# A two-layer decoder trunk: two adaptive-norm rounds moved to layer 1, one overflow loop, roots by threes

## The chip, the cores and the metric

The kernel runs on one core of a Trainium2 chip. The metric is the device time of one execution in microseconds (us). Engines: TensorE (PE in the rows; PEld is its weight load), VectorE (DVE), ScalarE (ACT), GpSimd (POOL), SyncE (SP). SP issues most loads and stores, ACT and POOL some.

## The reference

One sequence of 1,024 tokens, width 1,024, float32, two layers. Each layer takes shift, scale and gate for its two halves from a condition vector `c` ("adaptive norm": a matrix of 1,024 x 6,144 per layer). Layer 0's mixer joins a gated delta rule with a sparse attention that keeps the top 256 keys of each query; layer 1's is a gated linear attention. Behind each mixer stands a mixture of 32 experts, two for each token. At the end there is one more norm. Shortened:

```python
def reference(x, c, ...):
    for layer in range(2):
        shift1, scale1, gate1, shift2, scale2, gate2 = split(silu(c) @ ada_w[layer] + ada_b[layer], 6)
        h = rms_norm(x, norm_mix[layer]) * (1 + scale1) + shift1
        x = x + gate1 * (even_mixer(h) if layer == 0 else gla_mixer(h))
        h = rms_norm(x, norm_ffn[layer]) * (1 + scale2) + shift2
        x = x + gate2 * hier_moe(h)
    return rms_norm(x, final_norm)
```

## The kernel before

Tokens go in eight tiles of 128. A float32 product is made of three products of rounded parts: weights are loaded (`wraw`, `raw`), rounded on ACT (`whi`, `mhi`) and the rest formed on VectorE (`wlo`, `mlo`); TensorE then multiplies hi by hi, lo by hi and hi by lo (`mm3`, L112 to L114).

**Order.** Most of the program is written as generators that are advanced in turn, and a scheduler orders each engine's instructions from that; within an engine they run in that order, and waits for other engines are semaphores. Loads go in order of issue on the queue of their engine.

**Adaptive norm.** `ada_steps` (L263) works in rounds `(layer, g)`, g = 0, 1, 2, each a third of a layer's 6,144 columns: 16 tiles of 128 x 1,024 (`adaw`, 512 KB, loaded by POOL from `later`, L475, into two buffers), each multiplied in four matmuls (eight records in the trace) with `cond` at L283. At a round's start ACT loads the bias (L275); at its end VectorE adds it (L289), and for g > 0 ACT stores the row to `mods` in DRAM (L295), from where `gtf` is read later. Rounds (0,1), (0,2), (1,0), (1,1) and (1,2) run inside layer 0's projections (list at L473), one tile after each projected tile of rotary queries or keys. There VectorE and ACT also search the attention's thresholds bit by bit (`count`, L683 and L685; step at L701, L702), and VectorE applies the rotation (L494 to L497), TensorE turns the result (`tp`, L605) and ACT stores it (`qo`).

**Overflow loop.** Each expert takes 128 tokens in the main pass. What is over goes through a loop (L1703) whose count is read from the device. A turn fetches one expert's six weight parts by indirect loads on POOL (`fetch`, L1685), multiplies, and leaves `y`; the rows of `y` are scattered to `ybuf` (`scatter`, L1533) at the head of the next turn, with the indices `xic` kept from before, so the first turn's scatter carries none, and a second loop of at most one turn (L1719) makes the last scatter.

**Layer 1's norm stage** (`odd_mix`, L1787 to L1825). For each tile `combine` (L1740) loads the two expert rows (`yt`, 1 MB, four buffers), weighs and adds them (L1745 to L1748); `normalise` (L325, L328) makes `xn`, TensorE transposes it (L348) to `hh`, `hl`; `gate` multiplies it with the group `w3` of the weights, and two tiles later with `w0`. SP asks for `gtf`, then `yt`, then the weights of `w3`, whose rest `wlo` is formed on POOL (L370).

**The end** (`final`, L2060). Tile by tile: ACT scales (L2086), VectorE joins (L2090 to L2092), ACT squares (L2096), VectorE takes the root (eight short operations, L123 to L134) and multiplies (L2107); tile 6's product is on ACT and POOL (L2104, L2105). The order on these three engines is the order of the code.

Of the kernel before, what the change touches and what calls it, by code (L numbers as in the profile page):

```python
# [9 lines left out]
F32 = mybir.dt.float32  # L10
# [12 lines left out]
P = 128  # L23
# [4 lines left out]
NE = 32  # L28
# [59 lines left out]
class Trunk:  # L88
# [173 lines left out]

    def ada_steps(self, rounds, wp, pp, load, wait):  # L263

# [4 lines left out]
        for layer, g in rounds:  # L269
# [4 lines left out]
            for j in range(4):  # L274
                nc.scalar.dma_start(bias[32 * j:32 * j + 32].rearrange("p (u c) -> p u c", u=2), bcast(b2[j], 32))  # L275
            ps = pp.tile([P, 512], F32, name="ada", bufs=1)
            for u in range(2):
# [14 lines left out]
            if g:  # L292
# [3 lines left out]
                continue  # L296
            pt = pp.tile([P, 512], F32, name="ada", bufs=1)
            for c in range(4):
# [100 lines left out]
    def even_keep(self, st):  # L399
        nc = self.nc  # L400
        kp = self.pool(st, "keep0")
        self.cond = kp.tile([P, KD, 32], F32, name="cond")
        self.blk = kp.tile([P, 16], F32, name="blk")
# [16 lines left out]
    def even_inproj(self):  # L420
# [51 lines left out]
        self.rope_tables(hp)  # L472
        rounds = [(0, 1), (0, 2), (1, 0), (1, 1), (1, 2)]  # L473

# [933 lines left out]
    def moe(self, layer):  # L1408
        nc, tc, d = self.nc, self.tc, self.d
        tt, ts, stt, act, mm, tr = self.tt, self.ts, self.stt, self.act, self.mm, self.tr  # L1410
        with ExitStack() as st:
# [280 lines left out]
            y = y_tile()  # L1692
            nc.gpsimd.memset(ixc, 1 << 20)
            nc.gpsimd.memset(y, 0.0)
            for x in lw:
# [7 lines left out]
            with tc.For_i(0, nv, 1) as _:  # L1703
                scatter(y, ixc[:, 0:1])
                for n in range(2, 6):
                    fetch(n)
                x = all_tokens(xgs[0])
                w1 = take(0)
                p1 = up(x, w1)
                nc.vector.tensor_copy(ixc, ixn)  # L1710
                find()
                fetch(0)
                fetch(1)
                pick()
                p3 = up(x, take(1))
                h = hidden(gated(silu(p1), p3))
                down(h, take(2), y)
            any = nc.values_load(nx[0:1, 1:2], min_val=0, max_val=1)
            with tc.For_i(0, any, 1) as _:  # L1719
                scatter(y, ixc[:, 0:1])  # L1720
# [3 lines left out]
    def overflow(self, kp, sp):  # L1724
# [3 lines left out]
        xi = kp.tile([P, NE], I32, name="xi")  # L1728
        n = kp.tile([P, 2], I32, name="nx")
        ts(xb, self.base[:, NT], -1.0, 0.0, op0=OP.add, op1=OP.max)  # L1730
# [3 lines left out]
        nc.vector.tensor_tensor_scan(xc, self.ones[:, :NE], xb, 0.0, op0=OP.mult, op1=OP.add)  # L1734
        nc.vector.tensor_copy(n[:, :1], xc[:, NE - 1:NE])
        ts(n[:, 1:], xc[:, NE - 1:NE], 1.0, None, op0=OP.min)
        tt(xb, xc, xb, op=OP.subtract)
# [14 lines left out]
    def odd_mix(self):  # L1752
# [34 lines left out]
        with ExitStack() as sx:  # L1787
            xp = self.pool(sx, "x1p")
            junk = xp.tile([P, D], BF, name="junk")

            gt = xp.tile([P, D], F32, name="gtf")
            nc.sync.dma_start(gt, self.mod_row(0, 5))

            def tiles(ids):
                xs = [self.combine(xp, j, 4, gt) for j in ids]
                ys = [xp.tile([P, D], F32, name="xn", bufs=2) for _ in ids]
                self.normalise(xp, xs, junk, ys)
                return ys

            w3 = []  # L1800

            def get(i):
                if i:
                    yield from tiles((i, i + 1))
                    return
                yield from tiles((0,))
                w3.append(load(nc.gpsimd.tensor_tensor))
                with nullcontext():
                    yield from tiles((1,))

            norm = self.mixer_norm(1, get, xp, pp, "tp", hh, hl)
            next(norm)
            nc.scalar.dma_start(gn[:, :256], bcast(d["gla_out_norm"][0], P))
            nc.scalar.dma_start(gn[:, 256:], bcast(d["gla_out_norm"][0, :16], P))
            w0 = load()
            for i in range(NT + 2):
                if i % 2 == 0:
                    next(norm, None)
                if i < NT:
                    gate(3, w3[0], i)  # L1820
                if i >= 2:
                    gate(0, w0, i - 2)
                    nc.sync.dma_start(self.x2[(i - 2) * P:(i - 1) * P, :], self.xs[i - 2])
                if i == NT - 1:
                    ahead = load()  # L1825
        self.xst.close()
        before = self.rst
# [232 lines left out]
def final(k):  # L2060
# [3 lines left out]
    with ExitStack() as st:  # L2064
# [4 lines left out]
        gt = fp.tile([P, D], F32, name="gtf")  # L2069
        nc.sync.dma_start(gt, k.mod_row(1, 5))  # L2070
        yts = []
        for i in range(NT):
            yt = fp.tile([P, 2, D], F32, name="yt", bufs=NT)
            nc.sync.dma_start(yt, k.ybuf[i * 2 * P:(i + 1) * 2 * P, :].rearrange("(p k) d -> p k d", k=2))
            yts.append(yt)
        fn = fp.tile([P, D], F32, name="fng")
        p = pp.tile([P, D], F32, name="fn")
# [23 lines left out]
        def norm(i):  # L2101
            o = outs[i]
            if i == 6:
                k.act(o, k.xs[i], AF.Copy, scale=rs[:, i:i + 1])  # L2104
# [3 lines left out]
            nc.sync.dma_start(k.out[0, i * P:(i + 1) * P, :], o)  # L2108

        with k.tc.manual_schedule(engines={EN.DVE, EN.Activation, EN.Pool}):  # L2110
            scale(0)
            join(0)
            for i in range(NT):
                if i + 1 < NT:
                    scale(i + 1)
                square(i)
                root(i, i + 1)
                if i + 1 < NT:
                    join(i + 1)
                norm(i)  # L2120
    k.xst.close()
    k.rst.close()
# [28 lines left out]
```

## Time and profile before

| what | value |
|---|---|
| median of 3 runs | 2948.32 us (2944.62 to 2948.60) |
| the profiled execution | 2950.39 us, span 2948.7 us |
| granted TensorE clock, mean | 0.942 |
| TensorE busy | 2617.1 us, 89% |
| VectorE busy | 2218.7 us, 75% |
| ACT busy | 1690.3 us, 57% |
| POOL busy | 544.8 us, 18% |
| moved by DMA | 683.08 MB, mean 232 GB/s |

The span runs from the first to the last instruction. A busy share is a mean over stages; which engine sets the pace is read stage by stage. In the rows, "x8" is a count, `out<-in` names the tiles, and the bracket at a row's end is the engine's idle time before it and what ended that.

### The profile page before, as it was taken

How to read it: one execution, taken by the hardware profiler on the slowest of the kernel's cores; microseconds unless marked ns; L12 is line 12 of the kernel's file. 1: busy time of each engine (PE TensorE's matmuls, PEld its weight loads, DVE VectorE, ACT ScalarE, POOL GpSimd, SP SyncE). 2: the span in 40 equal slices, each digit the busy share in tenths (PEclk: the TensorE clock that was granted, in tenths of full speed). 3: DMA queues.
4: the chain of work that ended last, by engine and by line, in shares of the span. 5: the costliest groups of instructions: out<-in, count | busy, mean ns of one | idle time of the engine just before them, and what ended most of it. 6: DMA issues, size and time to landing. Idle time of an engine off the chain costs nothing. (4 is left out here: it accounts for less than half of the span.)

```text
span 2948.7 us, 46535 instructions
## 1 busy us (share of the span) xinstructions
PE 2617.1 (89%) x17622; PEld 2119.0 (72%) x17622; DVE 2218.7 (75%) x4055; ACT 1690.3 (57%) x2168; POOL 544.8 (18%) x511
## 2 busy tenths in 40 slices
PE   5999998877898899999997479999997999999980
PEld 3667887756687688888885367789786788888860
DVE  6777669577766899999986563483476999999866
ACT  4456653233444577777774456255433777777762
POOL 0100111232210122222223310002001122222220
PEclk8999999888999899999998779999997999999995
DMA  6345665422124799999994543444635899999964
GB/s 232 103 127 172 203 192 164 126 80 75 49 100 158 281 368 376 377 383 378 367 356 177 181 148 104 153 156 131 225 124 202 338 367 377 379 380 376 364 238 178
DMA packets 230569, 683.08 MB, mean 232 GB/s; under 512 B 50277, under 2 KB 128953, under 8 KB 176842
## 3 DMA queue, kind: packets, MB, share of 16 engines
q1 hardware_dynamic: 161696, 548.14, 50.8%
q0 software_dynamic: 37424, 107.01, 10.6%
q10 hardware_dynamic: 31226, 24.97, 2.6%
q8 instruction: 138, 2.26, 0.3%
q14 instruction: 85, 0.70, 0.1%
HBM read 628.07 MB, written 94.40 MB: 245 GB/s over the span
## 5 line engine op out<-in xcount | busy, mean ns | idle before, releaser
L1435 DVE TENSOR_TENSOR mlo<-raw,mhi 128x2048 fp32r<-128x2048 f32 (+1 forms) x420 | 915.1, 2194 | 96.0 <-ACT mhi L1434 94.8
L1434 ACT ACTIVATE mhi<-raw 128x2048 fp32r<-128x2048 f32 (+1 forms) x420 | 768.0, 1844 | 93.1 <-PE y L114 45.7
L112 PE MATMUL h<-mhi,xh 128*128 128x512 f32 x1072 | 434.2, 405 | 4.3 <-ACT xh L1496 2.7
L113 PE MATMUL h<-mlo,xh 128*128 128x512 f32 x1072 | 429.1, 400 | 4.6 <-DVE mlo L1435 4.6
L114 PE MATMUL h<-mhi,xl 128*128 128x512 f32 x1072 | 428.2, 399 | 0.0
L112 PE MATMUL pj<-whi,hh 128*128 128x256 f32 (+2 forms) x1088 | 325.5, 299 | 12.6 <-ACT hh L356 12.5
L114 PE MATMUL pj<-whi,hl 128*128 128x256 f32 (+2 forms) x1088 | 316.8, 291 | 4.1 <-DVE hl L357 4.1
L113 PE MATMUL pj<-wlo,hh 128*128 128x256 f32 (+2 forms) x1088 | 316.5, 291 | 0.0
L1483 POOL DMA_INDIRECT xg<-hbuf,tix x64 | 135.1, 2110 | 685.4 <-PE tp L1494 464.1
L113 PEld LDWEIGHTS h<-mlo,xh 128*128 128x128 f32 x1072 | 204.5, 191 | 52.5 <-DVE mlo L1435 6.7
L112 PEld LDWEIGHTS h<-mhi,xh 128*128 128x128 f32 x1072 | 204.7, 191 | 51.8 <-ACT xh L1496 4.0
L114 PEld LDWEIGHTS h<-mhi,xl 128*128 128x128 f32 x1072 | 204.2, 190 | 49.1 <-DVE xl L1497 0.9
L112 PEld LDWEIGHTS pj<-whi,hh 128*128 128x128 f32 x1088 | 210.7, 194 | 37.6 <-issue 18.1
L112 PE MATMUL y<-mhi,hh 128*128 128x512 f32 x536 | 224.2, 418 | 7.1 <-ACT mhi L1434 5.1
L113 PE MATMUL y<-mlo,hh 128*128 128x512 f32 x536 | 213.9, 399 | 3.4 <-DVE mlo L1435 3.4
L114 PEld LDWEIGHTS pj<-whi,hl 128*128 128x128 f32 x1088 | 209.7, 193 | 7.6 <-DVE hl L357 5.7
L114 PE MATMUL y<-mhi,hl 128*128 128x512 f32 x536 | 214.0, 400 | 0.9 <-DVE hl L1526 0.9
L113 PEld LDWEIGHTS pj<-wlo,hh 128*128 128x128 f32 x1088 | 210.7, 194 | 2.7 <-issue 1.3
L1533 POOL DMA_INDIRECT ybuf<-y,yix x64 | 145.6, 2276 | 195.7 <-ACT y L1545 169.2
L1496 ACT ACTIVATE xh<-tp 128x512 fp32r<-128x512 f32 x134 | 79.4, 597 | 124.6 <-PE tp L1494 124.6
L112 PE MATMUL pj<-hh,whi 128*128 128x512 f32 x320 | 130.0, 406 | 0.0
L370 DVE TENSOR_TENSOR wlo<-wraw,whi 128x512 fp32r<-128x512 f32 (+2 forms) x104 | 72.4, 708 | 75.4 <-ACT whi L369 75.1
(714 smaller groups left out, 5083.8 us busy)
## 6 DMA issues: line engine op xcount, KB each, us to landing
raw<-in_exp_w_dram SPq DMA_DIRECT2D x380, 1024.0 KB
adaw<-in_ada_w_dram POOLq DMA_DIRECT2D x80, 512.0 KB, 4.4
yt<-ybuf SPq DMA_DIRECT2D x16, 1024.0 KB
wraw<-in_even_w_in_dram SPq DMA_DIRECT2D x48, 256.0 KB
x<-in_x_dram SPq DMA_DIRECT2D x16, 512.0 KB
aw<-in_ada_w_dram SPq DMA_DIRECT2D x8, 1024.0 KB
hbuf<-th SPq DMA_DIRECT2D x16, 512.0 KB
x<-x SPq DMA_DIRECT2D x16, 512.0 KB
```

The lines of the kernel that those rows point to most:

```text
L112: self.mm(ps, ah, bh, start=first, stop=False)
L113: self.mm(ps, ah, bl, start=False, stop=False)
L114: self.mm(ps, al, bh, start=False, stop=last)
L370: (take or self.tt)(lo[:, ks, :cols], raw[:, :, :cols], hi[:, ks, :cols].bitcast(F32), op=OP.subtract)
L1434: act(h[:, us], raw[:, us], AF.Copy)
L1435: (take[u] if take else tt)(l[:, us], raw[:, us], h[:, us].bitcast(F32), op=OP.subtract)
L1483: return nc.gpsimd.indirect_dma_start(out=xg, out_offset=None, in_=self.hbuf, in_offset=bass.IndirectOffsetOnAxis(ap=it, axis=0), bounds_c ...
L1496: act(xh[:, us], as4(p), AF.Copy)
L1533: return nc.gpsimd.indirect_dma_start(out=self.ybuf, out_offset=bass.IndirectOffsetOnAxis(ap=iy, axis=0), in_=y, in_offset=None, bounds_ch ...
```

## The change

Rounds (1,1) and (1,2) leave layer 0's projections and run in layer 1's norm stage: six tiles are stepped after the first tiles of the norm have been put in the program, then three in each turn of the loop over tiles, the rest after it. `cond` moves to the pool that lives throughout; `yt` has three buffers instead of four. `w3` is loaded first in that stage, and split on VectorE. The overflow loop ends with its own scatter; the second loop, two memsets and a column of `nx` go. In `final` the first `yt` is asked for ahead of `gtf`, roots are taken for tiles 0 to 2, 3 to 5 and 6 to 7, and tile 5's product instead of tile 6's is on ACT and POOL.

```diff
@@ layer 0, projections
-        rounds = [(0, 1), (0, 2), (1, 0), (1, 1), (1, 2)]
+        rounds = [(0, 1), (0, 2), (1, 0)]
@@ overflow loop
             y = y_tile()
-            nc.gpsimd.memset(ixc, 1 << 20)
-            nc.gpsimd.memset(y, 0.0)
...
             with tc.For_i(0, nv, 1) as _:
-                scatter(y, ixc[:, 0:1])
                 for n in range(2, 6):
                     fetch(n)
...
                 down(h, take(2), y)
-            any = nc.values_load(nx[0:1, 1:2], min_val=0, max_val=1)
-            with tc.For_i(0, any, 1) as _:
                 scatter(y, ixc[:, 0:1])
@@ odd_mix
+            rounds = [(1, 1), (1, 2)]
+
+            def later(i):
+                x = xp.tile([P, 1024], F32, name="adaw", bufs=2)
+                nc.gpsimd.dma_start(x, self.ada_tile(i, rounds))
+                return x
+
+            ada = self.ada_steps(rounds, xp, pp, later, 0, "a", 3)
+            next(ada)
+
+            w3 = load()
             gt = xp.tile([P, D], F32, name="gtf")
             nc.sync.dma_start(gt, self.mod_row(0, 5))
 
             def tiles(ids):
-                xs = [self.combine(xp, j, 4, gt) for j in ids]
+                xs = [self.combine(xp, j, 3, gt) for j in ids]
...
-            w3 = []
-
             def get(i):
-                if i:
-                    yield from tiles((i, i + 1))
-                    return
-                yield from tiles((0,))
-                w3.append(load(nc.gpsimd.tensor_tensor))
-                with nullcontext():
-                    yield from tiles((1,))
+                return tiles((i, i + 1)) if i else itertools.chain.from_iterable(map(lambda j: tiles((j,)), (0, 1)))
 
             norm = self.mixer_norm(1, get, xp, pp, "tp", hh, hl)
             next(norm)
+            w0 = load()
+            for _ in range(6):
+                next(ada)
...
-            w0 = load()
             for i in range(NT + 2):
...
                 if i == NT - 1:
                     ahead = load()
+                for _ in range(3):
+                    next(ada, None)
+            run(ada)
@@ final
-        nc.sync.dma_start(gt, k.mod_row(1, 5))
...
             yts.append(yt)
+            if i == 0:
+                nc.sync.dma_start(gt, k.mod_row(1, 5))
...
-            if i == 6:
+            if i == 5:
...
+        after = {3: (root, 0, 3), 4: (norm, 0), 5: (norm, 1), 6: (norm, 2)}
         with k.tc.manual_schedule(engines={EN.DVE, EN.Activation, EN.Pool}):
             scale(0)
-            join(0)
             for i in range(NT):
                 if i + 1 < NT:
                     scale(i + 1)
+                join(i)
                 square(i)
-                root(i, i + 1)
-                if i + 1 < NT:
-                    join(i + 1)
+                if i in after:
+                    f, *j = after[i]
+                    f(*j)
+            root(3, 6)
+            for i in range(3, 6):
                 norm(i)
+            root(6, 8)
+            norm(6)
+            norm(7)
```

What this does to the order of instructions shows at three places. In layer 0's projections, TensorE: `pj` are the projection's matmuls, `tp` the transposes of the rotated tile, `ada` the adaptive norm's.

```order
 L114 MATMUL pj<-whi,hl 128x256
 L605 MATMUL tp<-ident,qa 128x128 x2
-L283 MATMUL ada<-adaw,cond 32x256 x4
 L112 MATMUL pj<-whi,hh 128x256
 L113 MATMUL pj<-wlo,hh 128x256
```

The four matmuls of one ada tile go; 32 such places are left out of this stretch.

POOL in the overflow loop, before; L1533 is the scatter, L1685 a fetch:

```order
L1533 DMA ybuf<-y,xic 2048x1024 [waits DMASW5_49,DMASW4_49,Pool_49]
L1685 DMA raw<-in_exp_w_dram,xw 128x2048 [waits DMASW6_49]
L1685 DMA raw<-in_exp_w_dram,xw 128x2048
L1685 DMA raw<-in_exp_w_dram,xw 128x2048 [waits DMASW0_49]
L1685 DMA raw_15477<-in_exp_w_dram,xw 128x2048 [waits DMASW1_49]
L1685 DMA raw<-in_exp_w_dram,xw 128x2048 [waits DMASW2_49,DVE_49,Activation_49]
L1685 DMA raw<-in_exp_w_dram,xw 128x2048 [waits DVE_49,Activation_49]
L1483 DMA xg_10377<-hbuf,xin 128x1024 [waits DVE_49,PE_49]
```

and with the change:

```order
L1685 DMA raw<-in_exp_w_dram,xw 128x2048 [waits DMASW5_49,Pool_49]
L1685 DMA raw<-in_exp_w_dram,xw 128x2048 [waits DMASW6_49,Pool_49]
L1685 DMA raw<-in_exp_w_dram,xw 128x2048 [waits DMASW7_49,Pool_49]
L1685 DMA raw_15262<-in_exp_w_dram,xw 128x2048 [waits DMASW0_49,Pool_49]
L1685 DMA raw<-in_exp_w_dram,xw 128x2048 [waits DMASW1_49,DVE_49,Activation_49]
L1685 DMA raw<-in_exp_w_dram,xw 128x2048 [waits DMASW2_49,DVE_49,Activation_49]
L1483 DMA xg_10163<-hbuf,xin 128x1024 [waits DMASW3_49,DVE_49,PE_49]
L1533 DMA ybuf<-y,xic 2048x1024 [waits DMASW4_49,Activation_49]
```

The scatter has gone from the head, where it waited for earlier POOL loads, to the foot, where it waits for ACT's `y`; the loop's closing branch, which waits for all loads and stores, comes right behind it.

TensorE at the start of layer 1's norm stage, before; `tp` transposes the first tile's `xn`, `pj` is its gate product:

```order
L348 MATMUL tp<-ident,xn 128x128 [waits DVE_49]
L348 MATMUL tp<-ident,xn 128x128 x7
L112 MATMUL pj<-whi,hh 128x260 [waits Activation_49]
L113 MATMUL pj<-wlo,hh 128x260 [waits Pool_49]
L114 MATMUL pj<-whi,hl 128x260 [waits DVE_49]
```

and with the change, from the end of the tenth ada tile on:

```order
L283 MATMUL ada<-adaw,cond 32x256 [waits DMASW6_49]
L283 MATMUL ada<-adaw,cond 32x256 x3
L283 MATMUL ada<-adaw,cond 32x256 [waits DMASW7_49]
L348 MATMUL tp<-ident,xn 128x128 [waits DVE_49]
L348 MATMUL tp<-ident,xn 128x128 x7
L283 MATMUL ada<-adaw,cond 32x256 x3
L283 MATMUL ada<-adaw,cond 32x256 [waits DMASW0_49]
L283 MATMUL ada<-adaw,cond 32x256 x3
L283 MATMUL ada<-adaw,cond 32x256 [waits DMASW1_49]
L283 MATMUL ada<-adaw,cond 32x256 x3
L112 MATMUL pj<-whi,hh 128x260 [waits Activation_49]
L113 MATMUL pj<-wlo,hh 128x260
```

The first thing that TensorE does there is now ten ada tiles, each behind its load; the transposes and the gate products of the first tiles stand between and behind further ada tiles, 22.25 of the 32 ahead of the third tile's `pj`. On POOL, 17 of the tile loads stand ahead of the first gate product `z`.

## Rows read from the trace of the kernel before

**Rows 1.** The page's slices, TensorE: busy tenths, 40 equal slices of the span.

```profile
PE   5999998877898899999997479999997999999980
```

**Rows 2.** Windows, layer 0's projections: us; busy PE, PEld, DVE, ACT, POOL; clock; DMA; GB/s.

```profile
390.00:410.00 20.00, 20.00 (x182) 17.01 (x184) 11.51 (x45) 13.34 (x25) 2.65 (x5) 1.00 0.58 166
...
470.00:490.00 20.00, 15.61 (x134) 11.30 (x126) 19.12 (x36) 2.31 (x6) 3.13 (x7) 0.91 0.58 174
...
sum 136.00, PE 128.45 PEld 108.48 DVE 106.85 ACT 57.87 POOL 15.85; mean PE 18.35 PEld 15.50 DVE 15.26 ACT 8.27 POOL 2.26
```

**Rows 3.** Timelines, layer 0's overflow loop: POOL, then ACT; start, duration, idle before, releaser.

```profile
1573.52 0.99 POOL L1533 DMA_INDIRECT ybuf<-y,yix  x1 [5.15 <-ACT y L1545]
1576.86 0.97 POOL L1533 DMA_INDIRECT ybuf<-y,xic  x1 [2.34 <-DMA ybuf<-y,yix]
1578.14 1.11 POOL L1685 DMA_INDIRECT raw<-in_exp_w_dram,xw  x1 [0.30 <-issue]
...
1605.58 1.06 ACT L1434 ACTIVATE mhi<-raw 128x1024 fp32r<-128x1024 f32 x1 [1.83 <-PEq L1703]
```

**Rows 4.** Timeline, SP, start of layer 1's norm stage.

```profile
1668.93 0.33 SPq L1792 DMA_DIRECT2D gtf<-mods  x1
...
1669.78 2.04 SPq L368 DMA_DIRECT2D wraw<-in_gla_w_in_dram  x3
```

**Rows 5.** Windows, layer 1's norm stage and the work behind it.

```profile
1669.00:1730.00 61.00, 16.85 (x76) 14.79 (x77) 48.29 (x89) 29.75 (x49) 9.65 (x6) 0.56 0.77 269
1730.00:1780.00 50.00, 48.94 (x391) 47.77 (x391) 23.24 (x51) 22.79 (x47) 12.84 (x16) 0.97 0.20 59
```

**Rows 6.** Timeline, TensorE, layer 1's norm stage, first transposes and third tile.

```profile
1691.58 1.97 PE L348 MATMUL tp<-ident,xn 128*128 128x128 f32 x8 [28.47 <-DMA wraw<-in_gla_w_in_dram]
...
1730.91 0.57 PE L112 MATMUL pj<-whi,hh 128*128 128x260 f32 x1
```

**Rows 7.** Timeline, VectorE, the end.

```profile
2888.88 1.28 DVE L2090 SCALAR_TENSOR_TENSOR yt<-yt,wts 128x1024 f32<-128x1024 f32 x1 [24.13 <-ACT yt L2086]
...
2893.91 0.15 DVE L123 TENSOR_SCALAR fr0y<-fss 128x1 f32<-128x1 f32 x1 [1.22 <-ACT fo L2096]
...
2895.44 1.28 DVE L2090 SCALAR_TENSOR_TENSOR yt<-yt,wts 128x1024 f32<-128x1024 f32 x1
...
2937.33 3.24 DVE L2092 TENSOR_TENSOR x<-x,yt 128x1024 f32<-128x1024 f32 x1
...
2943.45 1.28 DVE L2107 SCALAR_TENSOR_TENSOR fo<-x,frs,fng 128x1024 f32<-128x1024 f32 x1
```

**Rows 8.** Groups by line, TensorE, 366 to 470 us: count, busy us, mean ns, idle before.

```profile
L283 PE MATMUL ada<-adaw,cond 128*32 128x256 f32 x207 | 16.7, 393 | 3.1 <-DVE col L301 3.0 <-DMA adaw<-in_ada_w_dram 0.2
```

**Rows 9.** Timeline, TensorE, layer 0's projections, one period.

```profile
413.35 0.38 PE L605 MATMUL tp<-ident,qa 128*128 128x128 f32 x2
...
417.16 0.38 PE L605 MATMUL tp<-ident,qa 128*128 128x128 f32 x2
```

**Rows 10.** Groups by line, VectorE, 370 to 470 us.

```profile
L494 DVE TENSOR_TENSOR qa<-pj,cos 128x256 f32<-128x256 f32 x24 | 10.1, 420 | 9.0 <-DMA qbT<-qo 5.3 <-PE pj L114 2.7 <-ACT jka L685 0.8
```

**Rows 11.** SP at the second overflow loop's line in layer 1, and its next load.

```profile
L1719 SPq COMPARE_BRANCH  x3: 33/33/39, 2876.9 to 2880.6; - x3
...
2880.79 0.33 SPq L2070 DMA_DIRECT2D gtf<-mods  x1
```

**Rows 12.** DMA issues, 366 to 470, 450 to 492, 2300 to 2850 us: count, KB, landing us.

```profile
adaw<-in_ada_w_dram POOLq DMA_DIRECT2D x25, 512.0 KB, 4.1
...
adaw<-in_ada_w_dram POOLq DMA_DIRECT2D x10, 512.0 KB, 4.0
...
xg<-hbuf,tix POOLq DMA_INDIRECT x27, 9.2
```

**Rows 13.** Groups by line, POOL and VectorE, 1669 to 1740 us.

```profile
L370 POOL TENSOR_TENSOR wlo<-wraw,whi 128x520 fp32r<-128x520 f32 x4 | 8.2, 2078 | 14.0 <-DMA wraw<-in_gla_w_in_dram 12.3 <-ACT whi L369 1.7
...
L328 DVE TENSOR_SCALAR xn<-x,nrs 128x1024 f32<-128x1024 f32 x7 | 5.1, 746 | 0.0
```

More of the change, by code (lines that the diff above doesn't have):

```diff
@@ L261, in cond_setup, with ada_steps @@
         self.mods = self.dram.tile([2, 6 * D], F32, name="mods")
-    def ada_steps(self, rounds, wp, pp, load, wait):
+    def ada_steps(self, rounds, wp, pp, load, wait, tag="ada", bufs=1):
         nc, cp = self.nc, self.cp
@@ L275, in ada_steps @@
                 nc.scalar.dma_start(bias[32 * j:32 * j + 32].rearrange("p (u c) -> p u c", u=2), bcast(b2[j], 32))
-            ps = pp.tile([P, 512], F32, name="ada", bufs=1)
+            ps = pp.tile([P, 512], F32, name="ada", tag=tag, bufs=bufs)
             for u in range(2):
@@ L296, in ada_steps @@
                 continue
-            pt = pp.tile([P, 512], F32, name="ada", bufs=1)
+            pt = pp.tile([P, 512], F32, name="ada", tag=tag, bufs=bufs)
             for c in range(4):
@@ L401, in even_keep @@
         kp = self.pool(st, "keep0")
-        self.cond = kp.tile([P, KD, 32], F32, name="cond")
+        self.cond = self.cp.tile([P, KD, 32], F32, name="cond")
         self.blk = kp.tile([P, 16], F32, name="blk")
@@ L1728, in overflow @@
         xi = kp.tile([P, NE], I32, name="xi")
-        n = kp.tile([P, 2], I32, name="nx")
+        n = kp.tile([P, 1], I32, name="nx")
         ts(xb, self.base[:, NT], -1.0, 0.0, op0=OP.add, op1=OP.max)
@@ L1734, in overflow @@
         nc.vector.tensor_tensor_scan(xc, self.ones[:, :NE], xb, 0.0, op0=OP.mult, op1=OP.add)
-        nc.vector.tensor_copy(n[:, :1], xc[:, NE - 1:NE])
-        ts(n[:, 1:], xc[:, NE - 1:NE], 1.0, None, op0=OP.min)
+        nc.vector.tensor_copy(n, xc[:, NE - 1:NE])
         tt(xb, xc, xb, op=OP.subtract)
@@ L1819, in odd_mix @@
                 if i < NT:
-                    gate(3, w3[0], i)
+                    gate(3, w3, i)
                 if i >= 2:
```

## The prediction

> **What bounds the kernel now.** I read the page's slices first, then one table of windows for each stage that the change touches, then timelines inside these. TensorE is busy in nearly every slice [rows 1]; the three dips are the places between layers, at slice 22 to 23 (layer 0's overflow loop and layer 1's norm stage) and at the end. The change leaves both long expert stretches alone, so only four places count, and each has a limit of its own.
>
> *Layer 0's projections, 366 to 506 us.* TensorE has no gap in 390 to 410, VectorE has [rows 2]; from 470 it turns round, VectorE 19.12 of 20 and TensorE 15.61. So TensorE sets the pace first, VectorE (the threshold search and its masks) after.
>
> *Overflow loop.* It runs three times in layer 0 (three scatters of `ybuf<-y,xic` inside it, the first in [rows 3]) and not once in layer 1.
>
> *Layer 1's norm stage.* Its start is SP's `gtf` at 1668.93 [rows 4]. Until 1730 TensorE is busy 16.85 of 61 us at a granted clock of 0.56, waiting for the norm chain; from 1730 it is busy 48.94 of 50 [rows 5]. The change of limit is at 1730.91, the first `pj` of the third tile [rows 6].
>
> *The end.* VectorE works through eight tiles in a row and everything else follows it [rows 7].
>
> **Part 1: 32 ada tiles leave layer 0's projections.** The 207 records before 470 cost 16.7 us, 16.7 x 8/207 = 0.64 us for a tile's eight records [rows 8]; one sits in each TensorE period of 3.81 us (`tp` at 413.35 and at 417.16, [rows 9]). If TensorE alone set the pace, 16 us would go. VectorE's idle time speaks for it: `L494` waited 9.0 us in this stretch, and where a store of `qo` is named, the matmuls `pj` that it reads ended last, since TensorE had no gap there [rows 10]. Against the full gain: in the whole 136 us VectorE is busy 106.85 [rows 2], and it ends the stretch, so its own order (search, rope, masks) can take back a part. Bounds: -16 (all) and -3 (only the wait named for `pj`, 2.7). I take -11, nearer to the full gain, because the row without a gap is the first half of the stretch. Removed POOL issues, bias loads and stores of `mods` on ACT lie beside this and cost nothing.
>
> **Part 2: one overflow loop.** Before, the loop began with a scatter that waited 2.34 us for the last ordinary scatter, took 0.97, and the fetch behind it started at 1578.14 [rows 3]. Now the fetch is first: -3 in the first turn. The other two turns lose a scatter of 1.0 and 0.3 ahead of the fetch: -2.6. But the scatter now stands behind the turn's last `y`, and the loop's closing branch waits for it. A boundary took 1.83 us [rows 3]; a scatter needs 3.34 us from start to landing (1573.52 to 1576.86), so two boundaries get about 2 us longer, +4. On leaving, the second loop and its scatter go, -1. Sum -2.6, rounded to -3, bounds -6 and +2. The two memsets that go lay beside the experts' matmuls.
>
> **Part 3: the second loop of layer 1.** It is skipped, but SP spent 2876.9 to 2880.6 in it, and `gtf`, the first load of the end, follows at 2880.79 [rows 11]. All engines pass there, no work covers it: -3.9. Bounds -3.9 and 0 (if the wait only moves to the remaining loop).
>
> **Part 4: the same 32 tiles in layer 1's norm stage.** TensorE's order has 22.25 of them ahead of the third tile's `pj`, ten ahead of the first transposes. The idle TensorE has room for the matmuls, so the question is how fast tiles arrive. Two buffers: a tile is asked for when the tile two places earlier has been used, so two tiles take one landing plus one tile's matmuls. At clock 0.56 these take 0.64/0.56 = 1.1. Landing: 4.1 us in layer 0's projections [rows 12], 9.2 for POOL's 512 KB gathers beside saturated expert loads [rows 12]. I take 5.3, nearer to the first, since it is the same direct load, and raise it because the stage already has DMA engines busy 0.77 of the time and 269 GB/s [rows 5]. A tile then takes (5.3+1.1)/2 = 3.2, 22.25 tiles 71 us, against the 62 us that the stage had (1668.93 to 1730.91): +9. The other 9.75 tiles fall where TensorE has no gap: 9.75 x 0.64 = +6.4. In all +16. Bounds: with a landing of 4.1 a tile takes 2.6, the 22.25 are there in 58 us and only +6.4 is left; with 9.2 it is 5.15, 115 us, +59. The first weights asked for first, and their split on VectorE instead of POOL (8.2 us for four on POOL, [rows 13], beside which VectorE's own work stalled), go with this: SP now issues three weight loads ahead of the first `yt`, 2.04 us [rows 4], VectorE takes four splits of its own length and loses the stall; I cost both at nothing, because the first transposes wait for ten ada tiles (10 x 3.2 = 32 us), where they started 22.65 us into the stage (1691.58, [rows 6]). On POOL 17 tile issues stand ahead of the first gate product `z`; behind `z` waits only its store. ACT's bias loads and `mods` stores, some 16 issues, lie in a stage where ACT is busy 29.75 of 61 us [rows 5].
>
> The rows on VectorE show one more thing that touches POOL's loads: `L328`, SBUF to SBUF in f32, takes 746 ns for 1024 columns, less than 1.28 us for the two-input operation of the same size [rows 7, 13]. The Trainium skill (SBUF — State Buffer, the warning on the "DVE blocks DMA" trap) says that while VectorE runs such a two-port operation GpSimd can't write descriptors of the loads that it issues, and gives 620 ns growing to about 3,100. By that, as an estimate, a landing would be 2.5 us later, 7.8 in this stage, a tile 4.45, the part +44 and the kernel slower. The trace speaks against so much: the seven such operations here are 5.1 us in all, and while VectorE was busy 19.1 of 20 us in layer 0 the tiles still landed in 4.0 [rows 2, 12]. It stays as one cause of rival B.
>
> **Part 5: the end.** A period is 6.55 us (2888.88 to 2895.44): 3.8 for three operations, 1.22 waiting for ACT's square, 1.53 for the root's eight, or 1.28 for the norm in the wait's place. Before, 55.85 us from 2888.88 to the last norm's end at 2944.73 [rows 7]. After: 8 x 3.8 = 30.4; three roots of ten operations, about 1.9 each, 5.7; seven norms of 1.3, 9.1; one operation slowed by POOL's product beside it, +2.0 (3.24 instead of 1.22 at 2937.33). That is 47.2, so -8.7; the first `yt` comes one issue earlier, -0.4; stores in a closer row may cost some of it. I take -9, bounds -12 and -6.
>
> **Sum.** -11 -3 -3.9 +16 -9 = -10.9. The profiled execution took 2950.39 (span 2948.7), so 2939.5; it is 2.07 above the median 2948.32 of the runs, so the median should come to about 2938.
>
> **Rivals.** *A: the tiles hide.* Landing 4.1, part 4 only +6.4: sum -20.5, 2928. For it: the SP loads of the stage stop when norm buffers are full, so the DMA engines are less loaded than before; against it, 0.77 of them is a mean that already holds such pauses.
>
> *B: the tile loads become the norm stage's bound, and the kernel gets slower.* Place: TensorE before the third tile's `pj`. The other parts make -26.9, the late tiles +6.4, so the load chain must cost 20.5 for no change: 82.5 us for 22.25 tiles, 3.7 each, a landing of 6.3. From a landing of 6.85 (26.4 us late) it is slower by over 0.2%. Its price at 9.2 us is +59, 2980. For it: the order puts the tiles in front of the norm's own transposes, so each late tile also stops VectorE and ACT; SP's `yt` loads of 1 MB compete. Against it: 4.0 and 4.1 in layer 0's two stretches, beside DMA engines busy 0.58 of the time [rows 2, 12].
>
> *C: layer 0 gives nothing back.* The search on VectorE and ACT keeps its pace: part 1 only -3, sum -2.9, 2945.4, no change that shows. For it, VectorE's 19.12 of 20 at the stretch's end; against it, the gapless TensorE before.
>
> *D: the change does less than it says*: if leaving one loop costs what two did, part 3 is 0 and the time 2942; inside the forecast's range.
>
> **Chances.** Forecast 0.45 (with D), A 0.15, C 0.22, B 0.18. About 0.2% (5.9 us) is what a measurement of this kernel can tell from no change, so faster means below 2942.4. The forecast and A give faster, less 0.02 for the forecast's upper edge: 0.58. C and that edge give 0.24 for the same, B 0.18 for slower. The range 2925 to 2958 takes in A, C and B up to a landing of about 7.2; half of B and the corner where all gains are full are left out.
>
> **What would show it.** The third tile's first `pj` about 71 us after SP's `gtf` of that stage, with TensorE's waits for `adaw` between (A: 62; B: over 88). Layer 0's mask phase ends 11 us earlier (C: 3). In the overflow loop one scatter fewer at the loop's head, boundaries near 4 us. SP's first load of the end 3.9 us after the remaining loop's test would have ended, and the end about 47 us long on VectorE. The prediction is wrong if the `adaw` landing lies outside 4 to 7 us there, or if VectorE's order in layer 0 holds the old pace.

## The result, and the profile after

The changed kernel takes 2967.22 us (median of 4, 2964.16 to 2967.69) beside 2946.84 for the kernel before in the same comparison: a ratio of 1.0071, 95% interval 1.0055 to 1.0087. It is slower by some 20 us, where 9 to 10 us less were forecast; the range ended at 2958. The profiled execution took 2967.23 (span 2965.5, before 2948.7).

The page's slices of the changed kernel, TensorE and the GB/s moved:

```profile
PE   5999997877997999999997479999998899999991
...
GB/s 231 105 125 177 181 72 67 127 98 73 55 93 174 335 371 375 377 384 378 357 288 179 274 189 123 186 99 146 217 148 170 297 374 369 379 381 378 378 304 182
```

The GB/s of the kernel before, from its page:

```profile
GB/s 232 103 127 172 203 192 164 126 80 75 49 100 158 281 368 376 377 383 378 367 356 177 181 148 104 153 156 131 225 124 202 338 367 377 379 380 376 364 238 178
```

TensorE's dip has the same digits as in [rows 1], 7, 4 and 7 at slices 22 to 24. What differs is the DMA under it: 179, 274 and 189 GB/s in these slices, before 177, 181 and 148. To find where the 16.8 us of span went I cut both traces at the same events and took differences:

| stretch, from and to | before | after | difference |
|---|---|---|---|
| start to layer 0's last ordinary scatter | 1573.52 | 1560.34 | -13.2 |
| that scatter to SP's first load of layer 1 (the overflow loop) | 95.4 | 98.8 | +3.4 |
| SP's first load of layer 1 to layer 1's last ordinary scatter | 1201.8 | 1245.1 | +43.3 |
| that scatter to SP's first load of the end | 10.1 | 4.5 | -5.6 |
| SP's first load of the end to the span's end | 67.9 | 56.7 | -11.2 |

Three of the five gained what was forecast or more. The loop came out 6 us worse than its -3, and the norm stage, with what follows it, lost 27 more than its +16: that outweighs everything else.

*Layer 0's projections.* Windows of the changed kernel (busy PE, PEld, DVE, ACT, POOL, then clock, DMA share, GB/s):

```profile
390.00:410.00 20.00, 19.55 (x166) 19.37 (x166) 16.34 (x60) 13.63 (x29) 0.00 (x0) 1.00 0.30 86
...
430.00:450.00 20.00, 16.19 (x134) 15.50 (x133) 19.50 (x67) 10.34 (x21) 0.00 (x0) 1.00 0.20 54
...
470.00:490.00 20.00, 12.56 (x99) 12.15 (x99) 18.42 (x27) 2.80 (x6) 0.00 (x0) 0.86 0.53 155
```

Beside [rows 2], VectorE's busy time in 390 to 410 has gone from 11.51 to 16.34 of 20 and in 430 to 450, where it was 15.66, it is 19.50 already: it does the same work earlier, until it sets the pace itself. The last mask (`L737`) stands at 487.42 instead of 505.63.

*Overflow loop.* POOL's and ACT's timelines of its first turn:

```profile
1560.34 0.99 POOL L1533 DMA_INDIRECT ybuf<-y,yix  x1 [6.16 <-ACT y L1545]
...
1562.21 1.55 POOL L1685 DMA_INDIRECT raw<-in_exp_w_dram,xw  x1 [0.88 <-issue]
...
1588.91 1.01 POOL L1533 DMA_INDIRECT ybuf<-y,xic  x1 [5.65 <-ACT y L1545]
...
1594.61 1.03 POOL L1685 DMA_INDIRECT raw<-in_exp_w_dram,xw  x1 [4.68 <-issue]
```

```profile
1588.04 0.60 ACT L1545 ACTIVATE y<-y 128x512 f32<-128x512 f32 x1 [1.74 <-PE y L114]
...
1593.96 1.06 ACT L1434 ACTIVATE mhi<-raw 128x1024 fp32r<-128x1024 f32 x1 [5.33 <-PEq L1701]
```

The first fetch follows the ordinary scatter after 1.87 us, where it took 4.62 [rows 3]: -2.75, as forecast. But from ACT's last `y` (1588.04 + 0.60) to its next rounding of weights pass 5.33 us, where the boundary took 1.83 [rows 3]; at the second boundary it is 4.69, where it was 1.08. The scatter issued at 1588.91 lands 2.6 us later, and SP's semaphore operations of the closing branch (`L1701`) run from 1591.5 to 1593.7: the landing and the branch stand one behind the other. Fetch to fetch a turn is 32.4 us, before 29.4 (1578.14 to 1607.58).

*Layer 1's norm stage.* Windows, then TensorE's timeline, the waits (1659 to 1760, then 1768 to 1840), and the landing (from issue to the data's arrival) of the ada tiles issued in 1659 to 1700, 1700 to 1712 and 1712 to 1725:

```profile
1659.00:1700.00 41.00, 8.65 (x64) 1.61 (x64) 18.91 (x31) 13.73 (x19) 5.38 (x10) 0.50 0.99 374
1700.00:1750.00 50.00, 27.57 (x183) 16.00 (x184) 27.18 (x53) 16.42 (x28) 8.42 (x15) 0.70 0.82 274
...
1770.00:1800.00 30.00, 23.95 (x208) 20.66 (x208) 6.02 (x14) 8.38 (x19) 8.71 (x13) 1.00 0.45 138
```

```profile
1665.72 1.08 PE L283 MATMUL ada<-adaw,cond 128*32 128x256 f32 x8 [10.66 <-DMA adaw<-in_ada_w_dram]
...
1703.99 1.08 PE L283 MATMUL ada<-adaw,cond 128*32 128x256 f32 x8 [1.98 <-DMA adaw<-in_ada_w_dram]
...
1707.47 1.97 PE L348 MATMUL tp<-ident,xn 128*128 128x128 f32 x8
...
1751.95 0.58 PE L112 MATMUL pj<-whi,hh 128*128 128x260 f32 x1
```

```profile
PE ada L283 <- DMA adaw<-in_ada_w_dram: 58.7, 20, 10.7
...
PE ada L283 <- DMA adaw<-in_ada_w_dram: 6.4, 4, 2.8
```

```profile
adaw<-in_ada_w_dram POOLq DMA_DIRECT2D x10, 512.0 KB, 6.7
...
adaw<-in_ada_w_dram POOLq DMA_DIRECT2D x4, 512.0 KB, 4.5
...
adaw<-in_ada_w_dram POOLq DMA_DIRECT2D x2, 512.0 KB, 9.7
```

In the first 41 us the DMA engines are busy 0.99 of the time at 374 GB/s; before they were at 0.77 over the stage [rows 5] and at 0.82 in its first 31 us. A tile lands after 6.7 us there, and after 4.5 in the 12 us in which the engines have room. From 1712 on, when SP asks for more `yt`, it takes 9.7, and the median of all 23 loads issued ahead of the third tile's `pj` is 6.5. TensorE waits 58.7 us in all for `adaw`. The tenth tile is used 44.8 us into the stage and the first transposes start at 48.3, before at 22.65 [rows 6]; the third tile's `pj` is at 1751.95, 92.8 us into the stage, before 62.0. That is +30.8. The other 12.5 of the 43.3 come behind: the 9.75 tiles that are left take 6.2 us of matmuls (9.75 x 0.64) and 6.4 of waits. In 1770 to 1800 TensorE is busy 23.95 of 30, where before it had no gaps [rows 5].

The landing goes with the DMA engines and not with VectorE, as four windows of this stage show:

| tiles issued in | DMA share | VectorE busy, us | landing, us |
|---|---|---|---|
| 1659 to 1670 (4) | 0.91 | 2.10 of 11 | 7.0 |
| 1690 to 1700 (2) | 1.02 | 3.17 of 10 | 6.4 |
| 1700 to 1710 (2) | 0.59 | 0.93 of 10 | 4.1 |
| 1712 to 1725 (2) | 0.97 | 10.32 of 13 | 9.7 |

*Leaving layer 1's loop, and the end.* POOL's last scatter, SP's first load, VectorE's timeline, then POOL's product:

```profile
2904.26 0.99 POOL L1533 DMA_INDIRECT ybuf<-y,yix  x1 [6.90 <-ACTq L1701]
```

```profile
2908.77 0.33 SPq L2076 DMA_DIRECT2D yt<-ybuf  x1
```

```profile
2914.70 1.28 DVE L2094 SCALAR_TENSOR_TENSOR yt<-yt,wts 128x1024 f32<-128x1024 f32 x1 [17.50 <-ACT yt L2090]
...
2930.26 0.16 DVE L123 TENSOR_SCALAR fr0y<-fss 128x3 f32<-128x3 f32 x1
...
2932.13 1.28 DVE L2094 SCALAR_TENSOR_TENSOR yt<-yt,wts 128x1024 f32<-128x1024 f32 x1
...
2954.96 2.31 DVE L123 TENSOR_SCALAR fr6y<-fss 128x2 f32<-128x2 f32 x1
...
2959.07 2.48 DVE L2111 SCALAR_TENSOR_TENSOR fo<-x,frs,fng 128x1024 f32<-128x1024 f32 x2
```

```profile
2953.86 3.38 POOL L2109 TENSOR_TENSOR fo<-fo,fng 128x1024 f32<-128x1024 f32 x1 [48.62 <-DVE fo L2111]
```

The first load comes 4.5 us after the scatter began, before 10.1 [rows 11]. VectorE's work runs from 2914.70 to 2961.55, 46.85 us, where it took 55.85 [rows 7]; the root of three columns takes 1.87 (2930.26 to 2932.13). VectorE is still held once beside POOL's product: the first operation of the last root takes 2.31 us instead of 0.16, and the two end together (2957.24 and 2957.27).

### The profile page after: what moved, and what is told of

Same layout as the page of the kernel before. It is cut to its first block, busy times and chain, and to the rows that moved or that the text cites. A ratio compares the mean times of both kernels' runs of the same rounds, so it can differ in the third digit from the quotient of the medians.

```text
span 2965.5 us, 46323 instructions
## 1 busy us (share of the span) xinstructions
PE 2620.4 (88%) x17622; PEld 2119.4 (71%) x17622; DVE 2210.3 (75%) x4023; ACT 1690.7 (57%) x2168; POOL 533.8 (18%) x502
## 5 line engine op out<-in xcount | busy, mean ns | idle before, releaser
L1533 POOL DMA_INDIRECT ybuf<-y,yix x64 | 145.7, 2277 | 197.7 <-ACT y L1545 172.3
```

The costliest lines, as they stand in the source:

```text
L1533: return nc.gpsimd.indirect_dma_start(out=self.ybuf, out_offset=bass.IndirectOffsetOnAxis(ap=iy, axis=0), in_=y, in_offset=None, bounds_ch ...
```

## The experiments

Two theories stood first. *L*: the tiles' landings, in TensorE's row ahead of the norm's own work, hold the norm stage. *W*: the three `yt` buffers and the weights asked for first make it late. *M* puts the loss on the matmuls' TensorE time. *Q* says that the bytes on their way are what is short; later it stood against POOL's own pace. Medians are of each comparison's runs; the kernel before stood between 2940.8 and 2943.9 in these comparisons. "Layer 1" below is the table's third stretch; without ada tiles in the norm stage it took 1197.1 to 1202.4 us in five kernels (before, `ada_back`, `loop_only`, `hybrid`, `w3old`), mean 1200.8.

**ada_back.**

```diff
-        rounds = [(0, 1), (0, 2), (1, 0)]
+        rounds = [(0, 1), (0, 2), (1, 0), (1, 1), (1, 2)]
...
-            rounds = [(1, 1), (1, 2)]
...
-            ada = self.ada_steps(rounds, xp, pp, later, 0, "a", 3)
```

> The changed kernel with the 32 ada tiles put back into layer 0's projections; one overflow loop, the end and the first weights asked for first stay. Theory L (the tiles' landings, in TensorE's row ahead of the norm's own work, hold layer 1's norm stage): the stage (SP's first load there to the third tile's first pj) goes back from 92.8 to about 62 us, the 43 us of layer 1 are gone, layer 0 loses its 13: 2967 - 43 + 13 = about 2937. Rival W (three yt buffers and the weights asked for first make the stage late): the stage stays near 85, over 2955.

Measured: 2930.32 us, ratio to before 0.9945 (0.9923 to 0.9966). Layer 1 is 1197.1. The move alone makes the loss; the rest of the change is a gain. W falls.

**noload.**

```diff
             def later(i):
+                if i > 1:
+                    return kept[i % 2]
                 x = xp.tile([P, 1024], F32, name="adaw", bufs=2)
                 nc.gpsimd.dma_start(x, self.ada_tile(i, rounds))
+                kept.append(x)
                 return x
...
+            kept = []
```

> The changed kernel with 30 of the 32 adaw loads left out (all 32 tiles' matmuls stay and read the first two loaded tiles, so layer 1's mods are not the reference's). Theory L: the matmuls run in the idle start of the stage, the stage is about 62 us and nothing of the 43 us is left: about 2924. Rival M (the matmuls' TensorE time is what is paid): the stage's end still 20 us late, about 2944. Rival W: over 2950.

Measured: 2924.51 us, layer 1 1200.1. The ada matmuls of the stage by line, and where most of them stand:

```profile
L283 PE MATMUL ada<-adaw,cond 128*32 128x256 f32 x256 | 17.1, 419 | 11.3 <-DMA adaw<-in_ada_w_dram 11.3
```

```profile
1669.93 15.14 PE L283 MATMUL ada<-adaw,cond 128*32 128x256 f32 x246 [0.44 <-DMA adaw<-in_ada_w_dram]
```

All 256 records run, and TensorE waits only for the first landing (11.3 us, in the changed kernel 58.7 up to 1760). Its order is not the changed kernel's: with no loads to wait for, the scheduler put all 32 tiles in one block ahead of the transposes. So the run shows that the matmuls cost nothing where they stand in the idle start, and that without the loads, and the places the tiles take because of them, nothing of the 43 us is left. M falls for the idle start; behind the third tile's `pj` the changed kernel pays 6.2 us of matmuls.

**bufs3.**

```diff
-                x = xp.tile([P, 1024], F32, name="adaw", bufs=2)
+                x = xp.tile([P, 1024], F32, name="adaw", bufs=3)
```

> The changed kernel with three adaw buffers instead of two. Theory L, landing by latency: three tiles per landing of 6.4 plus 1.1, 2.5 us a tile instead of 3.75; the stage 15 to 25 us shorter: about 2947. Rival Q (the DMA engines' bytes are what is short): the landing grows with the number in flight to about 9, the tile stays near 3.5: within 5 us of 2967. TensorE's order has 30 tiles ahead of the third tile's pj here, which takes some of L's gain: 2947 to 2957.

Measured: 2950.52 us, ratio to before 1.0023 (1.0010 to 1.0037), 17 below the changed kernel; layer 1 1230.7. A window of the stage and the tiles' landing:

```profile
1670.00:1700.00 30.00, 10.21 (x80) 2.01 (x80) 16.81 (x28) 10.88 (x16) 4.75 (x9) 0.50 1.02 391
```

```profile
adaw<-in_ada_w_dram POOLq DMA_DIRECT2D x30, 512.0 KB, 6.5
```

A third tile on its way helps, inside the band that was given for L (by the two ratios to before it is 14 us, not 17). But the gain does not lie where L put it. The first transposes start 50.4 us into the stage with 14 tiles ahead of them, and the third tile's `pj` stands at 91.2 us (1744.09), in the changed kernel at 92.8. What changed is that 30 tiles, not 22.25, are done by then, and TensorE waits for none behind it. From the first tile's use to the fourteenth's it is 40.9 us (1661.40 to 1702.28), 3.1 a tile where L gave 2.5 and Q 3.5: the engines are full (1.02, 391 GB/s), and the third buffer takes a larger part of them. Neither theory holds alone in this stretch.

**late.** Each ada tile is queued on TensorE behind the last gate matmul (issue order only), none before the third tile.

```diff
+        self.lastmm = self.mm(ps, al, bh, start=False, stop=last)
...
-            for _ in range(6):
-                next(ada)
...
-                for _ in range(3):
-                    next(ada, None)
+                if i >= 2:
+                    with tc.issue_after(self.lastmm.ins):
+                        for _ in range(4):
+                            next(ada, None)
```

> The changed kernel with every ada tile queued on TensorE behind the third tile's gate product (issue order only), four in each turn after. The same loads and matmuls, no tile ahead of the norm's first work. Theory L: the stage is 62 us again, the 32 tiles cost their 20.5 us of TensorE time behind it: 2967 - 43 + 20.5 = about 2945. Rival Q: the loads still fill the stage's DMA engines, over 2955.

Measured: 2969.04 us, ratio 1.0079 (1.0057 to 1.0101): a miss. Layer 1 is 1249.9. The first transposes do start early again (32.5 us, 28.0 in `ada_back`). The loss has moved behind them; window and wait of `late`, then the same window of `ada_back`:

```profile
1740.00:1820.00 80.00, 64.13 (x528) 45.18 (x526) 13.90 (x24) 14.75 (x30) 23.38 (x39) 1.00 0.71 221
```

```profile
PE ada L283 <- DMA adaw<-in_ada_w_dram: 16.6, 19, 1.8
```

```profile
1740.00:1820.00 80.00, 79.68 (x468) 66.04 (x467) 35.28 (x52) 52.30 (x83) 10.80 (x14) 1.00 0.24 73
```

The stage itself is back: the third tile's `pj` is 64.0 us into it. Behind it 6 to 21 gate matmuls of 0.12 us stand between one tile and the next in TensorE's row, while with a landing of 4.9 us two buffers give a tile each (4.9 + 0.64)/2 = 2.8 us. TensorE loses 15.5 of 80 us there, the 16.6 that the wait names, on top of the 20.5 for the matmuls. Together that is 37 of the 49 us that layer 1 is above 1200.8; no row names the other 12. L in its first form, that only the place ahead of the norm matters, falls: the tiles hold TensorE wherever its row meets them faster than they arrive.

**late16.** As `late`, with round (1,2) alone moved and two tiles a turn.

```diff
+        rounds = [(0, 1), (0, 2), (1, 0), (1, 1)]
...
+            rounds = [(1, 2)]
...
+                if i >= 2:
+                    with tc.issue_after(self.lastmm.ins):
+                        next(ada, None)
+                if i >= 3:
+                    with tc.issue_after(self.lastmm.ins):
+                        next(ada, None)
```

> Only round (1,2), 16 tiles, moved; TensorE has two tiles in each turn behind the third tile's gate product (a turn is some 6 us of TensorE work there). If late missed because four tiles a turn stand closer than two buffers can be refilled, no waits are left here: layer 1 takes ada_back's 1197 plus 16 x 0.64 = 1207, layer 0 gives 5: about 2935. If tiles wait there whatever the spacing, over 2945.

Measured: 2955.94 us, ratio 1.0049 (1.0031 to 1.0067): a miss again. Layer 1 is 1222.8, and a wait is left:

```profile
PE ada L283 <- DMA adaw<-in_ada_w_dram: 6.3, 7, 2.9
```

16 tiles cost 22 in layer 1: 10.2 of matmuls, 6.3 of waits, 5.5 that no row names. Half the density halves the loss and does not remove it. Layer 0 gave nothing back here (its last store of `hbuf` at 938.2, inside the 930.4 to 939.8 of the kernels with all tiles there).

**half3.** Round (1,2) alone moved, at the head as in the change, three buffers.

```diff
+        rounds = [(0, 1), (0, 2), (1, 0), (1, 1)]
...
+            rounds = [(1, 2)]
...
+                x = xp.tile([P, 1024], F32, name="adaw", bufs=3)
```

> The changed kernel with only round (1,2), 16 tiles, moved, and three adaw buffers. Theory L: TensorE has 14 tiles ahead of the first transposes, (6.5+1.1)/3 = 2.5 us each, 36 us where they started after 22.7 us; the matmuls are hidden; the stage 5 to 13 us late, and layer 0 gives back half of its 13: 2929 to 2937. If the loads cost by their bytes alone (8.4 MB at 380 GB/s, 22 us): over 2940.

Measured: 2954.96 us, ratio 1.0040 (1.0025 to 1.0055): over the band, on the side of the bytes. TensorE at the fourteenth tile and the first transposes:

```profile
1713.65 1.08 PE L283 MATMUL ada<-adaw,cond 128*32 128x256 f32 x8 [2.52 <-DMA adaw<-in_ada_w_dram]
...
1714.66 1.97 PE L348 MATMUL tp<-ident,xn 128*128 128x128 f32 x8
```

The fourteenth tile is used 47.9 us into the stage (from 1665.74), 49.4 in `bufs3`; the third tile's `pj` is at 78.6 and layer 1 is 1215.0. So 14 tiles ahead of the transposes are enough to make the stage late. The traced execution took 2946.47, 8.5 less than the median; the trace does not show where the others spent that.

**yt1.**

```diff
-                xs = [self.combine(xp, j, 3, gt) for j in ids]
+                xs = [self.combine(xp, j, 1, gt) for j in ids]
```

> The changed kernel with one yt buffer instead of three, so that SP has 1 MB of yt on its way and not 3 MB. A look at one thing, the pace of the first eight ada tiles. If a tile's landing is set by what else is on its way at the full 400 GB/s, the eight take about 3 us each (24 us after the first landing) instead of 4.5; if it is POOL's descriptors or the two buffers alone, 4.5 stays. The whole kernel gets no faster, since the norm chain then waits for each yt: 2965 to 2990.

Measured: 2980.84 us (one run). From the first tile's use to the eighth's it takes 26.5 us (1659.88 to 1686.37), in the changed kernel 30.5 (1665.72 to 1696.19): 3.8 from one tile to the next instead of 4.4, between the two readings. Taking 2 of SP's 3 MB away gave a part.

**noyt.**

```diff
+        if i < 3:
             yt = sp.tile([P, 2, D], F32, name="yt", bufs=bufs)
             self.nc.sync.dma_start(yt, ...)
+            self.kept = getattr(self, "kept", []) + [yt]
+        yt = self.kept[i % 3]
```

> The changed kernel with five of the eight yt loads of layer 1's norm stage left out (tiles 3 to 7 add the rows of tiles 0 to 2 once more, so layer 1 works on other numbers and only the norm stage is read). TensorE's order in the stage is the changed kernel's. Ten ada tiles stood ahead of the first transposes, the tenth 44.8 us into the stage. If what SP has on its way sets the pace, the tiles go faster once the three yt are in (some 15 us): the tenth at 30 to 36 us. If the pace is POOL's own, the tenth stays at 42 to 46 us.

Measured: 2957.99 us (one run). The tenth tile is used 42.4 us into the stage, which is in the band given for POOL's own pace. The band was drawn wrong: without the five `yt` the weights, `gtf` and the three first `yt` still fill the engines until 1690 (a DMA share of 0.96 in 1680 to 1690). What the run does show is the landing at either load. Windows, POOL's issues and TensorE's use of two tiles:

```profile
1670.00:1680.00 10.00, 3.24 (x24) 0.60 (x24) 9.12 (x15) 7.79 (x11) 1.38 (x3) 0.50 1.02 358
...
1700.00:1710.00 10.00, 4.96 (x35) 2.00 (x36) 9.06 (x16) 5.32 (x9) 1.81 (x4) 0.67 0.64 212
```

```profile
1673.47 0.53 POOL L1793 DMA_DIRECT2D adaw<-in_ada_w_dram  x1 [1.20 <-PE ada L283]
...
1701.32 0.53 POOL L1793 DMA_DIRECT2D adaw<-in_ada_w_dram  x1 [5.14 <-PE ada L283]
```

```profile
1680.40 1.08 PE L283 MATMUL ada<-adaw,cond 128*32 128x256 f32 x8 [1.05 <-DMA adaw<-in_ada_w_dram]
...
1705.38 0.74 PE L283 MATMUL ada<-adaw,cond 128*32 128x256 f32 x8 [3.53 <-DMA adaw<-in_ada_w_dram]
```

The tile issued at 1673.47, with the engines full (1.02), is used 6.9 us later; the one issued at 1701.32, at 0.64, after 4.1. VectorE is as busy in the one window as in the other (9.12 and 9.06 of 10). In this pair too the landing follows the DMA engines, not VectorE.

**sp_queue.**

```diff
-                nc.gpsimd.dma_start(x, self.ada_tile(i, rounds))
+                nc.sync.dma_start(x, self.ada_tile(i, rounds))
```

> The changed kernel with the adaw loads issued by SP instead of POOL, where they stand in one row with yt and the weights; TensorE's order then has four tiles ahead of the first transposes and not ten. If POOL's writing of descriptors beside a busy VectorE made the landing long, it falls to about 4 us in the stage's first 40 us; if the bytes on their way did, it stays at 6 to 8 there. Either way fewer tiles stand in front of the norm: the first transposes at 30 to 35 us, the kernel 10 to 25 us faster than the changed one, 2942 to 2957.

Measured: 2945.29 us, ratio 1.0009 (0.9995 to 1.0024); layer 1 1220.3. SP's issue of the third and fourth tile, and TensorE:

```profile
1670.96 0.96 SPq L1790 DMA_DIRECT2D adaw<-in_ada_w_dram  x2
```

```profile
1677.63 2.31 PE L283 MATMUL ada<-adaw,cond 128*32 128x256 f32 x16 [13.24 <-DMA adaw<-in_ada_w_dram]
...
1684.56 1.97 PE L348 MATMUL tp<-ident,xn 128*128 128x128 f32 x8 [4.62 <-DVE xn L328]
```

From 1670.96 to 1677.63 it is 6.7 us although SP issues them, at 326 GB/s in 1670 to 1680: a load need not come from POOL to land late. In SP's queue these loads also stand behind `yt` and weights, so this run alone does not say what held them. The first transposes start 28.7 us into the stage, since SP's own row now holds `yt` and tiles in turn and the scheduler put four tiles ahead of them.

**loop_only and hybrid.** The one overflow loop on the kernel before (its edit is the change's own); and `ada_back` with the loop pair of before in layer 0 alone:

```diff
+                if layer == 0:
+                    scatter(y, ixc[:, 0:1])
                 for n in range(2, 6):
                     fetch(n)
...
+                if layer == 1:
+                    scatter(y, ixc[:, 0:1])
+            if layer == 0:
+                any = nc.values_load(nx[0:1, 1:2], min_val=0, max_val=1)
+                with tc.For_i(0, any, 1) as _:
+                    scatter(y, ixc[:, 0:1])
```

> The kernel before with the one overflow loop alone. By the changed kernel's trace layer 0's loop is 3.4 us longer (the landing of the scatter and the loop's closing branch stand one behind the other) and leaving layer 1's is 5.6 shorter: -2 us against before, about 2942 beside 2944. The prediction's own sum for it was -3 -3.9 = -7, about 2937.

> ada_back with the loop pair of before (scatter at the head, second loop) in layer 0 alone, the one loop in layer 1. If a turn of the one loop costs 3 us more where turns are made, layer 0's loop goes from 100 back to about 95: 3 to 5 us below ada_back, about 2926. Rival: the turns cost the same and the trace's difference is scatter between executions: 2930.

Measured: `loop_only` 2946.92 us, ratio 1.0012 (0.9999 to 1.0026), no difference that shows, against the prediction's -7; the -2 expected here lies just outside the interval too. Its trace has +5.0 in layer 0's loop and -4.1 at the second loop's place. `hybrid` 2925.51, ratio 0.9942 (0.9923 to 0.9960), has the lowest median of all that leave nothing out. It is 4.8 below `ada_back`, but by the two ratios to before only about 1, so the times do not show what the loop pair is worth in layer 0. The traces do, in part: layer 0's loop, from the ordinary scatter to SP's next load, takes 95.4 us before and 95.5 in `hybrid` (1564.32 to 1659.79), and 98.1 to 102.3 in the twelve kernels with the one loop, 99.7 on their mean. POOL in `hybrid`:

```profile
1564.32 0.99 POOL L1533 DMA_INDIRECT ybuf<-y,yix  x1 [5.23 <-ACT y L1545]
...
1568.93 1.12 POOL L1685 DMA_INDIRECT raw<-in_exp_w_dram,xw  x1 [0.31 <-issue]
```

The fetch comes 4.6 us after the scatter again, and the loop as a whole is shorter all the same.

**w3old.** `ada_back` with the first weights, POOL's split and four `yt` buffers as before.

```diff
-            w3 = load()
...
+                xs = [self.combine(xp, j, 4, gt) for j in ids]
...
+                w3.append(load(nc.gpsimd.tensor_tensor))
```

> ada_back with the weights' first load, its split on POOL and four yt buffers as before. Shows what 'weights asked for first' is worth without ada tiles in the way: the prediction said nothing. Theory: VectorE loses the stall beside POOL's split, 2 us; 2930 to 2934. Rival W': the new order costs: below 2928.

Measured: 2933.92 us, ratio 0.9973 (0.9957 to 0.9988), beside 2930.32 and 0.9945 (0.9923 to 0.9966); layer 1 is 1202.1 there, 1197.1 and 1200.7 in the two with the weights first. All three readings lean to the new order, but the intervals overlap: a gain is not shown, and a cost (W') still less.

## Why the prediction was wrong, point by point

- **Part 1** (layer 0, -11, bounds -16 and -3) holds. This trace has -13.2. Over all traces layer 0's last store of `hbuf` is at 935.0 us on the mean of the five kernels with all tiles in layer 0 and at 923.4 on the mean of seven without the 32: -11.6. TensorE did set the pace first and VectorE after it: the last mask came 18.2 us earlier, and part of that was lost again behind it. Rival C falls.
- **Part 2** (layer 0's loop, -3) was wrong in sign, +3.4 here and +4.3 on the mean of twelve kernels (99.7 beside 95.4). The step that failed is "two boundaries get about 2 us longer": it took the landing (3.34) and the branch (1.83) as one beside the other. They follow each other: the two boundaries took 5.33 and 4.69 us instead of 1.83 and 1.08, +7.1 where +4 stood in the sum. The other 3 us of the miss are not traced to a row here.
- **Part 3** (-3.9) was -5.6 here; over the thirteen kernels with one loop in layer 1 the gap is 4.5 to 6.3 instead of 10.1, so -3.8 to -5.6. Rival D falls.
- **Part 5** (-9) was -9.0 in VectorE's own work and -11.2 from SP's first load on, since VectorE starts 5.9 us after that load (2908.77 to 2914.70), where it took 8.1, and the last stores did not cost more.
- **Part 4** (+16) is the failure, +43.3, and rival B is what happened. The mechanism was right and is quoted in B: TensorE waits before the third tile's `pj`. Two terms were mis-sized. The landing, "I take 5.3, nearer to the first", measured 6.7 in the first 41 us and 6.5 over all loads ahead of the third tile's `pj`. With 6.7 the same rule gives (6.7 + 1.1)/2 = 3.9 a tile and 87 us to that `pj`; 92.8 were measured. The rule's 1.1 is short as well: a tile is asked for 1.4 us after the first matmul of the one two places earlier (1673.91 to 1675.32). The other term, "the other 9.75 tiles fall where TensorE has no gap: 9.75 x 0.64", left out that there too a tile has to arrive: 12.5 instead of 6.4.
- The reason given for 5.3 was a DMA share of 0.77 over the stage. The stage's head alone, at 0.82, would not have warned either, since in 370 to 390 tiles landed in 4.1 us beside a share of 0.80. What was put at nothing is the tiles' own bytes. From 1659 to 1752 the changed kernel moved 29.08 MB, from 1669 to 1731 the kernel before 16.44:

```profile
DMA packets 9990, 29.08 MB, mean 313 GB/s; under 512 B 1144, under 2 KB 4864, under 8 KB 8960
```

```profile
DMA packets 6018, 16.44 MB, mean 265 GB/s; under 512 B 640, under 2 KB 3840, under 8 KB 4992
```

The most that one of the table's windows above shows is 405 GB/s (1690 to 1700). At that rate 29.08 MB take 72 us, an estimate from these rows: the 71 us of the forecast would have left the DMA engines no pause at all.
- The prediction gave B its place, its price and its point (a landing over 6.85), and a chance of 0.18; 6.7 with the late tiles' waits was enough. Of its two signs the `pj` told (92.8, "B: over 88"); the landing's bounds, 4 to 7, did not, since 6.7 lies inside. The range should have reached B's middle.
- On the Trainium skill's warning (SBUF — State Buffer, the "DVE blocks DMA" trap): the trace does not show it here. A tile issued while VectorE was busy 9.06 of 10 us was used 4.1 us later, tiles issued while it was busy 2.10 of 11 and 3.17 of 10 landed after 7.0 and 6.4, and loads that SP issued took 6.7. That rule's estimate, +44 (its own terms give +43), came near the measured size for another reason.

What stays open: what 12 of the 49 us in `late` and 5 of the 22 in `late16` are (some 0.3 us a tile in both), and how much of layer 0's gain half the tiles bring (`half3` and `late16` differ by 6 us there, and the five kernels alike in layer 0 by 9).

## What to carry to other kernels

Work that moves into a stage with idle TensorE brings its loads with it: add their bytes to what the stage moves already, and divide by the highest rate that a window of the trace shows, before a landing is taken from a stage with room. Here that alone gives 72 us for a stage of 62. In an engine's fixed order a load that comes late stops everything behind it, so the question for each moved tile is how far apart the row meets them, against one landing divided by the buffers. At the end of a loop that closes with a branch on every load and store, a store put last is paid in full in each turn.

## What the runs showed that was not expected

- The landing of the same 512 KB load went from 4.0 to 4.1 us (DMA share 0.57 to 0.80 in layer 0) to 6.7 (0.99), and a single tile in the head of the stage took 8.8 to its use (issued 1687.43, used 1696.19).
- A third buffer brought tiles faster in the full stretch (3.1 us from use to use beside 4.3) but the third tile's `pj` no earlier; all but 2 us of its gain in layer 1 lie behind it.
- Taking out a loop that makes no turn gave 3.8 to 5.6 us at its place (10.1 against 4.5 to 6.3 from the last scatter to SP's next load).
- POOL's product of 3.38 us stood beside a VectorE operation of 128 x 2 elements that took 2.31 us instead of 0.16; before it had added the same 2 us to one of 128 x 1024 [rows 7].
